# A decoder block's prologue: which engine takes four low parts of the second token block, and where a sum of two weighed conditioning rows stands on GpSimd

## The chip, the cores and the metric

The kernel runs on one core of one Trainium2 chip. A core has TensorE (PE in the profile, its weight loads PEld), VectorE (DVE), ScalarE (ACT), GpSimd (POOL) and SyncE (SP, which here issues the DMA transfers in one queue, in order). The metric is the device time of one execution in microseconds (us), the median of several runs.

## The reference, cut to what matters

```python
mod = jax.nn.silu(c) @ w_cond[l] + b_cond[l]          # c: (1, 1024), w_cond: (1024, 6 * 1024)
shift_m, scale_m, gate_m, shift_f, scale_f, gate_f = [m[:, None, :] for m in jnp.split(mod, 6, axis=-1)]
h = rmsnorm(x, g_mix_pre[l]) * (1.0 + scale_m) + shift_m      # x: (1, 2048, 1024)
proj = h @ w_in[l]                                            # q, k, v: 512 columns each, u: 512
attn = stick_breaking_attention(q, k, v)                      # 8 heads of 64
pool = pooling_mixer(u, w_pool[l], pool_scale[l])             # trailing means over 2, 4, 8, 16 tokens
x = x + gate_m * rmsnorm(concatenate([attn, pool]) @ w_out[l], g_mix_post[l])
h = rmsnorm(x, g_ffn_pre[l]) * (1.0 + scale_f) + shift_f
x = x + gate_f * rmsnorm((silu(h @ w_gate[l]) * (h @ w_up[l])) @ w_down[l], g_ffn_post[l])
```

Everything is float32. The change lies in the first 100 us: in the making of `h` for the second of four blocks of 512 tokens, and in the sums that give the six parts of `mod`.

## The kernel before

**Stages.** A prologue (about 200 us) makes the conditioning parts, turns and modulates the tokens and makes q, k, u and v of the first token blocks; then come the attention with the rest of the projections woven in, the output projection, and the feed-forward part. The order on PE, ACT, DVE and POOL is the order in which the code is written (a manual schedule); SP issues DMAs in order too, each after its own waits, so a DMA that waits holds up those behind it.

**Products in two parts.** A float32 operand x is split into a rounded high part and a low part, x minus the high part. A product takes three passes on PE: high by high, high by low, low by high. `tokens(tb, k)` gives the two parts of token block `tb` for chunk `k`, 128 of the 1024 input columns. For block 1 the parts of chunks 0 to 3 lie in the tile `ht1a` and those of chunks 4 to 7 in `ht1b`.

**Block 1.** `turn1(kc)` has PE turn four 128x128 pieces (L600, tile `x`) and calls `modulate(1, kc, ...)`: ACT writes the high part (L586) and then the unrounded value `h` (L588), and one subtraction makes the low part (L591). Which engine does L591 is the last argument: GpSimd where one is given, else GpSimd for even kc and VectorE for odd. `first_products(n, 1, ...)` multiplies them for the first three chunks of w_in (n = 0, 1, 2: q0, k0, q1): the passes with high parts at L612, those with the low parts at L614. The loop goes over the pairs of chunks (0, 1), (2, 3), (4, 5), (6, 7), and behind each of the first two n it calls `turn1` for a chunk of the next pair, `run_small` (a small task, such as a step of the pooling of `u`) and a step of the conditioning sums.

**Conditioning.** `rest_of_cond` does parts 3, 4, 2 and 5 of `mod`. For each, `cond_sums` loads eight pieces of 128x1024 (`wc`, four buffers, for chunks 0 to 5; two slots of the tile `spare` for chunks 6 and 7), weighs and adds the first six on VectorE (L213 for chunk 0, L215 for the others, into `acc`), and weighs the other two on ACT (L260). GpSimd adds those two into `spare[:, 1]` (L262), 128x1024. `cond_end` runs as a second generator beside the next part's `cond_sums`: it lets two steps pass, adds `spare[:, 1]` into `acc` on VectorE (L271), and goes on to the columns or gate rows.

**Around it on VectorE.** Between the steps stand the first pooling task of `u`: two copies of 16 columns (L376, L377), a sum `us` (L382), and `um` in three instructions (L393, L396, L397). `um` is stored by a DMA from SP (L398, `mtd`); the next load of a `wc` piece is issued behind it in SP's queue.

Of the kernel before, what the change touches and what calls it, by code (L numbers as in the profile page):

```python
# [12 lines left out]
ALU = mybir.AluOpType  # L13
# [7 lines left out]
KC = D // P  # L21
# [22 lines left out]
def block_kernel(ctx, tc, x, c, w_cond, b_cond, g_mix_pre, g_mix_post, w_in, w_pool,  # L44
                 pool_scale, w_out, g_ffn_pre, g_ffn_post, w_gate, w_up, w_down, out):
    nc = tc.nc
# [6 lines left out]
    def raw(ap):  # L53
        return ap.bitcast(F32)
# [151 lines left out]
    def cond_load(part, kc, wc):  # L206
        nc.sync.dma_start(wc, wc_rows[:, kc, part * D:(part + 1) * D])
        return wc

    def cond_step(acc, kc, wc):  # L210

        if kc == 0:
            nc.vector.tensor_scalar_mul(acc, wc, cs[:, 0:1])  # L213
        else:
            nc.vector.scalar_tensor_tensor(acc, wc, cs[:, kc:kc + 1], acc, ALU.mult, ALU.add)  # L215

    def new_wc(name):
        return cond.tile([P, D], F32, tag="wc", bufs=4, name=name)
# [4 lines left out]
    def column_part(acc, part, dst):  # L223
        ps = t_ps(f"cp{part}").rearrange("p (c n) -> p c n", n=64)
        for kc in range(KC):
            nc.tensor.matmul(ps[:, kc], acc[:, kc * P:(kc + 1) * P], ones[:, 0:64],
                             start=True, stop=True)
        nc.vector.tensor_tensor(dst, ps[:, :, 0], colv[:, part * KC:(part + 1) * KC], ALU.add)

    def plus_one_times(dst, g0):  # L230
        nc.vector.scalar_tensor_tensor(dst, dst, 1.0, colv[:, g0:g0 + KC], ALU.add, ALU.mult)

    def gate_part(acc, part, g_post, dst):

        hi, lo = (tokp.tile([P, D], F32R, tag=tag, name=f"gs{part}{tag}") for tag in ("xt", "xs"))
        split(hi, lo, acc)
        g = spare[:, 2 + part // 5]
        nc.sync.dma_start(g, g_post.partition_broadcast(P))
        for _ in range(4):
            yield  # L240
        for half in range(2):
            cols = slice(half * TB, (half + 1) * TB)
            ps = z_ps(f"gp{part}_{half}")
            nc.tensor.matmul(ps, ones_r, hi[:, cols], start=True, stop=False)
            nc.tensor.matmul(ps, ones_r, lo[:, cols], start=False, stop=True)
            nc.vector.tensor_tensor(g[:, cols], g[:, cols], ps, ALU.mult)
        nc.sync.dma_start(dst, g)

    last_sum = {}

    def cond_sums(part, acc):
        if part in (2, 5):
            b = cond.tile([1, D], F32, tag="brow", bufs=1, name=f"br{part}")
            nc.sync.dma_start(b, b_cond[0:1, part * D:(part + 1) * D])
        for n, kc in enumerate((0, 1, 2, 3, 6, 7, 4, 5) if part == 3 else range(KC)):
            wc = cond_load(part, kc, new_wc(f"wc{part}_{kc}") if kc < 6 else spare[:, kc - 6])
            if kc < 6:
                cond_step(acc, kc, wc)
            else:
                nc.scalar.mul(wc, wc, cs[:, kc:kc + 1])  # L260
            if n == KC - 1:
                nc.gpsimd.tensor_tensor(spare[:, 1], spare[:, 1], spare[:, 0], ALU.add)  # L262
                last_sum[part] = spare[:, 1]
            if kc == 0 and part in (2, 5):
                nc.vector.tensor_tensor(acc[0:1, :], acc[0:1, :], b, ALU.add)
            yield

    def cond_end(part, acc):
        yield
        yield  # L270
        nc.vector.tensor_tensor(acc, acc, last_sum.pop(part), ALU.add)  # L271
        for _ in range(1 if part in (2, 5) else 4):
            yield
        if part in (2, 5):
            yield from gate_part(acc, part, *((g_mix_post, gmd) if part == 2 else (g_ffn_post, gfd)))
        else:
            column_part(acc, part, mods["bf" if part == 3 else "af"])
            if part == 4:
                plus_one_times(mods["af"], 56)

    def rest_of_cond():

        end = iter(())
        for part in (3, 4, 2, 5):
            acc = new_acc(part)
            for _ in cond_sums(part, acc):
                next(end, None)
                yield
            for _ in end:
                pass  # L290
            end = cond_end(part, acc)
        for _ in end:
            yield
# [19 lines left out]
    def tokens(tb, k, cols=slice(0, TB)):  # L313
        if tb == 1:
            both = ht[1][k // HK]
            return both[:, 0, k % HK, cols], both[:, 1, k % HK, cols]
        return ht[tb][0][:, k, cols], ht[tb][1][:, k, cols]
# [263 lines left out]
    def modulate(tb, kc, src, low=None):  # L581

        hi, lo = tokens(tb, kc)
        a, b = mods["am"][:, kc:kc + 1], mods["bm"][:, kc:kc + 1]
        h32 = tokp.tile([P, TB], F32, tag="h32", bufs=4, name=f"h{tb}_{kc}")
        nc.scalar.activation(hi, src, AF.Identity, bias=b, scale=a)  # L586
        if tb:
            nc.scalar.activation(h32, src, AF.Identity, bias=b, scale=a)  # L588
        else:
            nc.vector.tensor_scalar(h32, src, a, b, ALU.mult, ALU.add)  # L590
        (low or (nc.gpsimd, nc.vector)[kc % 2]).tensor_tensor(lo, h32, raw(hi), ALU.subtract)  # L591
# [5 lines left out]
    def turn1(kc):  # L597
        pt = t_ps(f"x1_{kc}")
        for j in range(4):
            nc.tensor.transpose(pt[:, j * P:(j + 1) * P], early1[j][:, kc * P:(kc + 1) * P], ident)  # L600
        modulate(1, kc, pt, nc.gpsimd if kc < 3 else None)

    first_ps, lead = {}, []
    first_banks = {(0, 0): mm_only, (3, 0): av_ps, (0, 1): av_ps, (1, 1): mm_only}
# [88 lines left out]
    spare = hc.tile([P, 4, D], F32, tag="hi", name="spare")  # L693
# [9 lines left out]
    first_products(0, 0, 6, 7)  # L703
    first_products(1, 0, 6, 7)
    turn1(0)
    run_small()
    next(rest)
    first_products(2, 0, 6, 7)
    turn1(1)
    run_small()  # L710
    next(rest)
# [5 lines left out]
    for ks in pairs:  # L717
        for n in range(3):
            first_products(n, 1, *ks)
            if n < 2 and ks[0] < 6:  # L720
                turn1(ks[0] + 2 + n)
            run_small()
            if n < 2:
                next(rest)
            if (n, ks[0]) == (0, 6):
                loaded.append(chunk_load(chunks[4], 0))
# [1037 lines left out]
```

## Time and profile before

| what | value |
|---|---|
| median of 3 runs | 2288.1 us (2287.57 to 2288.57) |
| the profiled execution's own time | 2286.46 us, 1.6 us below the median |
| its span in the trace | 2284.5 us, so 2.0 us lie around it |
| mean granted TensorE clock | 0.998 of full speed |
| busy: PE, DVE, ACT, POOL | 2246.8 (98%), 1622.1 (71%), 1164.2 (51%), 1293.0 us (57%) |
| PE busy from 62 to 82 us | 16.48 of 20.00 us |
| PE busy from 82 to 240 us | 157.99 of 158.00 us |

A line of the timeline reads: start in us from the start of the span, duration in us, engine, line of the kernel, operation, output tile <- input tiles, shapes, count, and in brackets the idle time of the engine before it with what ended it. Instructions of one line that follow each other are merged into one row with their count. A line of the list of waits reads: who waited <- for whom, sum in us, times, longest. The chain of work that ended last is a list of start, duration and what was on the chain. Line numbers are those of the kernel before, if not said otherwise; in the kernel after they are smaller by two to four.

### The profile page before, as it was taken

What the parts mean: (1) busy time and instruction counts of PE and PEld (TensorE: products, weight loads), DVE (VectorE), ACT (ScalarE), POOL (GpSimd) and SP (SyncE); (2) the same over time, 40 slices, a digit from 0 to 9 for tenths busy, and PEclk for the clock granted to TensorE, in tenths of its full rate; (3) what the DMA queues carried; (4) which work ended last, traced back from release to release, by engine and by line L of the source; (5) the groups of instructions that cost most, each with busy time, mean ns of one, the idle gap of its engine ahead of it and who ended that gap; (6) DMA issues with size and microseconds to landing.
All of it is one profiled execution on the core that took longest, in us unless ns stands there. A gap on an engine that the chain in (4) does not pass through costs nothing.

```text
span 2284.5 us, 33020 instructions
## 1 busy us (share of the span) xinstructions
PE 2246.8 (98%) x10597; PEld 1842.0 (81%) x10597; DVE 1622.1 (71%) x2243; ACT 1164.2 (51%) x2412; POOL 1293.0 (57%) x1592
## 2 busy tenths in 40 slices
PE   7999999999999999999999999999999999999998
PEld 4788888888888778888888888888888888888886
DVE  7774569999999957666655566787766566655557
ACT  4434569899998855443232323554533323234444
POOL 4342257787778855546777777331576665651004
PEclk9999999999999999999999999999999999999999
DMA  8886764443435536665555555776854333328564
GB/s 313 284 280 204 279 174 117 115 105 105 122 111 158 169 113 220 221 223 171 164 157 161 158 160 185 269 243 206 264 166 131 99 112 96 111 92 301 193 197 143
DMA packets 307081, 405.14 MB, mean 177 GB/s; under 512 B 19222, under 2 KB 179546, under 8 KB 303836
## 3 DMA queue, kind: packets, MB, share of 16 engines
q1 hardware_dynamic: 302444, 400.15, 54.8%
q10 hardware_dynamic: 4464, 2.88, 0.4%
q8 instruction: 83, 1.36, 0.3%
q14 instruction: 90, 0.74, 0.1%
HBM read 274.51 MB, written 128.45 MB: 176 GB/s over the span
## 4 chain that ended last, share of the span: by engine, by line
PE 85%; DVE 9%; DMA 1%; issue 1%; POOL 1%; ACT 1%; SPq 0%; POOLq 0%; DVEq 0%; ACTq 0%
DVE pr L871 5%; PE t_g L68 4%; PE t_u L69 4%; PE t_g L69 4%; PE t_u L68 4%; PE t_g L70 3%; PE t_u L70 3%; PE dn0p L69 3%; PE dn0p L68 3%; PE dn0p L70 3%; PE wt L888 3%; PE dn1p L68 3%; PE dn1p L69 3%; PE dn1p L70 3%; PE b_u L70 3%; PE b_u L69 3%
## 5 line engine op out<-in xcount | busy, mean ns | idle before, releaser
L877 POOL TENSOR_TENSOR w<-sg,pr 128x512 f32<-128x512 f32 (+2 forms) x320 | 307.9, 962 | 38.9 <-DVE pr L871 27.2
L1279 POOL TENSOR_TENSOR s<-s,cu 128x512 f32<-128x512 f32 x88 | 131.4, 1500 | 239.4 <-DVE cu L1278 146.4
L871 DVE TENSOR_TENSOR_SCAN pr<-pr,carry,begin 128x512 f32<-128x512 f32 x192 | 243.6, 1269 | 0.0
L858 ACT ACTIVATE sg<-z 128x512 f32<-128x512 f32 (+2 forms) x320 | 185.0, 578 | 46.8 <-PE z L856 33.2
L59 DVE TENSOR_TENSOR wtl<-wt,wth 128x512 fp32r<-128x512 f32 (+1 forms) x320 | 188.0, 588 | 18.2 <-ACT wth L58 17.9
L58 ACT CAST wth<-wt 128x512 fp32r<-128x512 f32 (+1 forms) x320 | 183.8, 575 | 13.5 <-PE wt L888 13.5
L860 ACT ACTIVATE pr<-z 128x512 f32<-128x512 f32 (+2 forms) x320 | 184.2, 576 | 0.0
L888 PE MATMUL wt<-ident,w 128*128 128x128 f32 x1088 | 174.2, 274 | 4.7 <-POOL pr L868 2.6
L59 DVE TENSOR_TENSOR u_s_l<-u_s,u_s_h 128x512 fp32r<-128x512 f32 x66 | 64.3, 975 | 146.1 <-ACT u_s_h L58 146.1
L888 PEld LDWEIGHTS wt<-ident,w 128*128 128x128 f32 x1088 | 134.7, 140 | 36.8 <-POOL pr L868 3.9
L1269 ACT ACTIVATE s<-s 128x512 f32<-128x512 f32 x88 | 55.7, 633 | 182.2 <-DVE s L1268 182.2
L903 PE MATMUL av<-wth,vt 128*128 128x512 f32 (+1 forms) x320 | 128.9, 403 | 0.8 <-ACT o L908 0.5
L59 DVE TENSOR_TENSOR u_a_l<-u,u_a_h 128x512 fp32r<-128x512 f32 x66 | 73.9, 1121 | 69.3 <-ACT u_a_h L58 69.3
L904 PE MATMUL av<-wtl,vt 128*128 128x512 f32 (+1 forms) x320 | 119.3, 373 | 3.3 <-DVE wtl L59 2.8
L69 PE MATMUL dn0p<-w0p_l,g0p_h 128*128 128x512 f32 x308 | 120.7, 392 | 0.0
L855 PE MATMUL z<-kt,qt 128*128 128x512 f32 (+2 forms) x320 | 118.4, 370 | 2.1 <-ACT pr L860 2.0
L68 PE MATMUL dn0p<-w0p_h,g0p_h 128*128 128x512 f32 x308 | 120.5, 391 | 0.0
L70 PE MATMUL dn0p<-w0p_h,g0p_l 128*128 128x512 f32 x308 | 120.3, 391 | 0.0
L856 PE MATMUL z<-kt,qt 128*128 128x512 f32 (+2 forms) x320 | 117.1, 366 | 0.0
L69 PE MATMUL dn1p<-w1p_l,g1p_h 128*128 128x512 f32 x292 | 114.4, 392 | 0.0
L68 PE MATMUL dn1p<-w1p_h,g1p_h 128*128 128x512 f32 x292 | 114.2, 391 | 0.0
L70 PE MATMUL dn1p<-w1p_h,g1p_l 128*128 128x512 f32 x292 | 114.1, 391 | 0.0
(659 smaller groups left out, 7050.2 us busy)
## 6 DMA issues: line engine op xcount, KB each, us to landing
g<-in_w_gate_dram SPq DMA_DIRECT2D x42, 512.0 KB, 4.7
u<-in_w_up_dram SPq DMA_DIRECT2D x42, 512.0 KB, 5.2
wc<-in_w_cond_dram SPq DMA_DIRECT2D x32, 512.0 KB, 8.1
qt<-qd SPq DMA_DIRECT2D x64, 256.0 KB, 4.0
wd<-in_w_down_dram SPq DMA_DIRECT2D x44, 256.0 KB, 2.9
tdt<-wd SPq DMA_DIRECT2D x44, 256.0 KB, 2.0
w0p<-tdt SPq DMA_DIRECT2D x44, 256.0 KB, 3.5
w1p<-tdt SPq DMA_DIRECT2D x44, 256.0 KB, 2.9
```

Source lines behind the costliest of these rows:

```text
L58: nc.scalar.copy(hi, src)
L59: low.tensor_tensor(lo, src, raw(hi), ALU.subtract)
L68: nc.tensor.matmul(ps, lh, rh, start=first and i == 0, stop=False)
L69: nc.tensor.matmul(ps, lh, rl, start=False, stop=False)
L70: nc.tensor.matmul(ps, ll, rh, start=False, stop=last and i == n - 1)
L858: nc.scalar.activation(sg[:, 0:L], z[:, 0:L], AF.Sigmoid, scale=0.125)
L860: nc.scalar.activation(pr[:, 0:L], z[:, 0:L], AF.Sigmoid, scale=-0.125)
L871: nc.vector.tensor_tensor_scan(pr[:, 0:L][:, ::-1], pr[:, 0:L][:, ::-1], begin[:, TB - L:][:, ::-1], zero if carry is None else carry, ALU ...
L877: nc.gpsimd.tensor_tensor(w[:, 0:L], sg[:, 0:L], pr[:, 1:L + 1], ALU.mult)
L888: nc.tensor.transpose(wt[:, i * P:(i + 1) * P], wss[u][i][:, b * P:(b + 1) * P], ident)
L903: nc.tensor.matmul(av[:, lo0:], vb, wh[:, lo0:], start=first, stop=False)
L1279: nc.gpsimd.tensor_tensor(s, s, u, ALU.mult)
```

## The change

The low part (L591) of every chunk of block 1 but chunk 7 is made by GpSimd: chunks 3 and 5 go over from VectorE. The sum of the two weighed pieces (L262) is no longer written by the last step of `cond_sums` but by the first step of `cond_end`, which runs right behind the first step of the next part.

```diff
@@ -246,8 +246,6 @@
-    last_sum = {}
-
     def cond_sums(part, acc):
...
                 nc.scalar.mul(wc, wc, cs[:, kc:kc + 1])
-            if n == KC - 1:
-                nc.gpsimd.tensor_tensor(spare[:, 1], spare[:, 1], spare[:, 0], ALU.add)
-                last_sum[part] = spare[:, 1]
             if kc == 0 and part in (2, 5):
                 nc.vector.tensor_tensor(acc[0:1, :], acc[0:1, :], b, ALU.add)
             yield
 
     def cond_end(part, acc):
+        nc.gpsimd.tensor_tensor(spare[:, 1], spare[:, 1], spare[:, 0], ALU.add)
         yield
         yield
-        nc.vector.tensor_tensor(acc, acc, last_sum.pop(part), ALU.add)
+        nc.vector.tensor_tensor(acc, acc, spare[:, 1], ALU.add)
...
-        modulate(1, kc, pt, nc.gpsimd if kc < 3 else None)
+        modulate(1, kc, pt, nc.gpsimd if kc != 7 else None)
```

The next two lists are GpSimd's rows from chunk 2 of block 1 on, before and after. `h_2` is the unrounded value of chunk 2 and so on, `spare<-spare` is the sum of the two weighed pieces (of part 3, then of part 4), `wk_0_l` the low part of a weight chunk.

```order
L591 TENSOR_TENSOR ht1a<-h_2_721,ht1a 128x512
L262 TENSOR_TENSOR spare<-spare 128x1024
L591 TENSOR_TENSOR ht1b<-h_4_776,ht1b 128x512
L591 TENSOR_TENSOR ht1b<-h_6_825,ht1b 128x512
L59 TENSOR_TENSOR wk_0_l<-wk_0_32_869,wk_0_h 128x256 x2
L262 TENSOR_TENSOR spare<-spare 128x1024
L59 TENSOR_TENSOR wk_0_l<-wk_0_32_869,wk_0_h 128x256 x2
```

The same place on GpSimd after the change:

```order
L587 TENSOR_TENSOR ht1a<-h_2_721,ht1a 128x512
L587 TENSOR_TENSOR ht1a<-h_3_744,ht1a 128x512
L264 TENSOR_TENSOR spare<-spare 128x1024
L587 TENSOR_TENSOR ht1b<-h_4_776,ht1b 128x512
L587 TENSOR_TENSOR ht1b<-h_5_800,ht1b 128x512
L587 TENSOR_TENSOR ht1b<-h_6_825,ht1b 128x512
L59 TENSOR_TENSOR wk_0_l<-wk_0_32_869,wk_0_h 128x256 x4
L264 TENSOR_TENSOR spare<-spare 128x1024
```

Chunks 3 and 5 came in; part 3's sum now stands behind chunk 3, and part 4's sum behind all four low parts of the weight chunk instead of between them. The sums of parts 2 and 5 keep their places.

VectorE's rows from the last weighed piece of part 3 (`acc_614<-wc_5`) to the third of part 4 (`acc_752<-wc_2`), before:

```order
L215 SCALAR_TENSOR_TENSOR acc_614<-wc_5_729,cs,acc_614 128x1024
L591 TENSOR_TENSOR ht1a<-h_3_745,ht1a 128x512
L376 COPY u_0_705<-halo_230 128x16
L377 COPY halo_230<-u_0_705 128x16
L213 TENSOR_SCALAR acc_752<-wc_0_753,cs 128x1024
L382 TENSOR_TENSOR us_0_1_763<-u_0_705 128x527
L393 SCALAR_TENSOR_TENSOR um_0_780<-us_0_1_763,u_0_705 128x512
L396 TENSOR_TENSOR uf_782<-us_0_1_763,rcnt 128x2
L397 TENSOR_TENSOR um_0_780<-uf_782,u_0_705 128x2
L215 SCALAR_TENSOR_TENSOR acc_752<-wc_1_786,cs,acc_752 128x1024
L591 TENSOR_TENSOR ht1b<-h_5_800,ht1b 128x512
L215 SCALAR_TENSOR_TENSOR acc_752<-wc_2_804,cs,acc_752 128x1024
```

And after:

```order
L215 SCALAR_TENSOR_TENSOR acc_614<-wc_5_729,cs,acc_614 128x1024
L372 COPY u_0_705<-halo_230 128x16
L373 COPY halo_230<-u_0_705 128x16
L213 TENSOR_SCALAR acc_751<-wc_0_752,cs 128x1024
L378 TENSOR_TENSOR us_0_1_763<-u_0_705 128x527
L389 SCALAR_TENSOR_TENSOR um_0_780<-us_0_1_763,u_0_705 128x512
L392 TENSOR_TENSOR uf_782<-us_0_1_763,rcnt 128x2
L393 TENSOR_TENSOR um_0_780<-uf_782,u_0_705 128x2
L215 SCALAR_TENSOR_TENSOR acc_751<-wc_1_786,cs,acc_751 128x1024
L215 SCALAR_TENSOR_TENSOR acc_751<-wc_2_804,cs,acc_751 128x1024
```

The two subtractions are gone and nothing else moved on VectorE: behind these rows stand, as before, the sum into `acc` (L271), the piece `wc_3` of part 4 (L215) and the low part of chunk 7 (L591). PE, ACT and SP have the same rows in the same order.

## The prediction

> **What bounds the kernel now.** First the page's head: PE is busy nearly all the time, so only what makes PE wait counts.
>
> ```profile
> span 2284.5 us, 33020 instructions
> PE 2246.8 (98%) x10597; PEld 1842.0 (81%) x10597; DVE 1622.1 (71%) x2243; ACT 1164.2 (51%) x2412; POOL 1293.0 (57%) x1592
> ```
>
> Then PE's waits up to 240 us, and busy time by stretch (columns: stretch, length, then busy us of PE, PEld, DVE, ACT, POOL, clock, DMA share, GB/s). The change touches the second and third of these waits. After 82 us PE has none for 158 us, so what shifts PE at 82 us shifts all that follows.
>
> ```profile
> PE x_pt L537 <- DVE x_v L119: 5.1, 1, 5.1
> PE first L614 <- DVE ht1a L591: 2.9, 1, 2.9
> PE first L614 <- DVE ht1b L591: 0.6, 2, 0.4
> 62.00:82.00 20.00, 16.48 (x82) 12.62 (x80) 16.21 (x20) 10.67 (x16) 6.95 (x5) 1.00 0.85 295
> 82.00:240.00 158.00, 157.99 (x732) 130.92 (x733) 98.23 (x160) 64.28 (x141) 52.91 (x52) 1.00 0.78 256
> ```
>
> Third, PE's timeline: it waits 2.91 us for chunk 3's low part, 0.40 for chunk 5's, 0.23 for chunk 7's.
>
> ```profile
> 67.48 0.39 PE L614 MATMUL first<-ht1a,wq_h 128*128 128x512 f32 x1
> 70.78 0.50 PE L614 MATMUL first<-ht1a,wq_h 128*128 128x512 f32 x1 [2.91 <-DVE ht1a L591]
> ...
> 76.48 0.50 PE L614 MATMUL first<-ht1b,wq_h 128*128 128x512 f32 x1 [0.40 <-DVE ht1b L591]
> ...
> 81.39 0.39 PE L614 MATMUL first<-ht1b,wq_h 128*128 128x512 f32 x1
> 82.01 0.50 PE L614 MATMUL first<-ht1b,wq_h 128*128 128x512 f32 x1 [0.23 <-DVE ht1b L591]
> ```
>
> Fourth, the chain that ended last, which decides. It does not pass through the 2.91 us wait. It runs from a load of part 4 (issued at 64.64) over VectorE (L213 to L397) to the store of `um`, the load of `wc_3` issued behind that store, its L215 and chunk 7's low part, to PE at 82.01.
>
> ```profile
> 64.64 6.61 DMA wc<-in_w_cond_dram
> 71.28 0.75 DVE acc L213
> ...
> 73.48 1.16 DVE um L397
> 74.66 0.33 SPq L398
> ...
> 75.08 4.25 DMA wc<-in_w_cond_dram
> 79.42 1.37 DVE acc L215
> 81.28 0.69 DVE ht1b L591
> ```
>
> Last, GpSimd and VectorE at that place, and ACT's `h` of chunks 3, 4 and 5.
>
> ```profile
> 66.51 2.37 POOL L262 TENSOR_TENSOR spare<-spare 128x1024 f32<-128x1024 f32 x1
> 73.28 1.33 POOL L591 TENSOR_TENSOR ht1b<-h,ht1b 128x512 fp32r<-128x512 f32 x1 [4.40 <-ACT h L588]
> 78.98 1.29 POOL L591 TENSOR_TENSOR ht1b<-h,ht1b 128x512 fp32r<-128x512 f32 x1 [4.37 <-ACT h L588]
> 68.84 1.28 DVE L215 SCALAR_TENSOR_TENSOR acc<-wc,cs,acc 128x1024 f32<-128x1024 f32 x1 [2.65 <-DMA wc<-in_w_cond_dram]
> 70.04 0.68 DVE L591 TENSOR_TENSOR ht1a<-h,ht1a 128x512 fp32r<-128x512 f32 x1
> 70.91 0.18 DVE L377 COPY halo<-u 128x16 f32<-128x16 f32 x1
> 73.48 1.15 DVE L397 TENSOR_TENSOR um<-uf,u 128x2 f32<-128x2 f32 x1
> 77.55 1.21 DVE L271 TENSOR_TENSOR acc<-acc,spare 128x1024 f32<-128x1024 f32 x1
> 79.42 1.93 DVE L215 SCALAR_TENSOR_TENSOR acc<-wc,cs,acc 128x1024 f32<-128x1024 f32 x1 [0.67 <-DMA wc<-in_w_cond_dram]
> 66.05 0.77 ACT L588 ACTIVATE h<-x,bm,am 128x512 f32<-128x512 f32 x1
> 72.43 0.77 ACT L588 ACTIVATE h<-x,bm,am 128x512 f32<-128x512 f32 x1
> 74.26 0.77 ACT L588 ACTIVATE h<-x,bm,am 128x512 f32<-128x512 f32 x1
> ```
>
> The sum on GpSimd (66.51 to 68.88) fills the time in which VectorE waits for a load until 68.84; there it disturbs nobody.
>
> **The two engines hold each other up.** Rows where they overlap:
>
> ```profile
> 59.15 2.20 DVE L215 SCALAR_TENSOR_TENSOR acc<-wc,cs,acc 128x1024 f32<-128x1024 f32 x1
> 60.63 1.88 POOL L591 TENSOR_TENSOR ht1a<-h,ht1a 128x512 fp32r<-128x512 f32 x1 [0.36 <-ACT h L588]
> 61.87 1.72 DVE L215 SCALAR_TENSOR_TENSOR acc<-wc,cs,acc 128x1024 f32<-128x1024 f32 x1
> 142.10 2.40 POOL L262 TENSOR_TENSOR spare<-spare 128x1024 f32<-128x1024 f32 x1 [1.86 <-ACT spare L260]
> 142.53 2.00 DVE L377 COPY halo<-u 128x16 f32<-128x16 f32 x1 [1.68 <-ACT u L369]
> ```
>
> A copy that takes 0.18 us alone took 2.00 and ended at 144.53, just behind GpSimd's sum (144.50). The L215 of 61.87 ended 1.08 us behind GpSimd's subtraction (62.51); GpSimd's of 60.63 ended 1.16 behind the L215 that ended at 61.35. L397 took 1.15 and ended with chunk 4's subtraction (73.28 + 1.33 = 74.61). So the later one waits for the earlier one's end, then takes 1.08 (L215) or 1.16 (a subtraction), and one that waits goes ahead of the other engine's next. The Trainium skill, SBUF — State Buffer, "Who interferes with whom", says that a VectorE instruction with two SBUF inputs and a GpSimd instruction that reads SBUF block each other for the whole instruction, whichever issues first winning; read strictly, the loser then needs its whole time (1.28, not 1.08), which for the two L215 blocked below would make the forecast some 0.2 us later. The trace has the block and the shorter remainder.
>
> **The change, part by part.**
>
> *Chunk 3 to GpSimd.* Its `h` ends at 66.82, GpSimd is free (66.51), and starts 0.08 later as for chunk 4 (`h` ends 73.20, start 73.28): 66.90, plus 1.3, is 68.21. PE follows 0.06 later, as now (70.72 to 70.78): 68.27 instead of 70.78. Gain at this point 2.51; the wait shrinks to 0.4.
>
> *The sum one place later* starts at 68.17 and ends at 70.54 (2.37). VectorE's L215 of `wc_5`, whose load releases it at 68.84, now meets it and ends at 70.54 + 1.08 = 71.62 instead of 70.12.
>
> *Chunk 4.* PE is 2.51 earlier, so its `h` makes GpSimd ready at 73.28 − 2.51 = 70.77; it waits for that L215, and ends at 71.62 + 1.16 = 72.78. VectorE's first copy of 16 columns waits for that and ends near 72.8.
>
> *Chunk 5 to GpSimd.* Its `h` ends at 75.03 − 2.51 = 72.52, so GpSimd starts at once behind chunk 4 and ends near 74.03. PE reaches this product at 73.57 (76.48 − 0.40 − 2.51) and goes on at 74.09: it is now 2.39 ahead. The second copy, ready at 72.9, waits behind chunk 5 too and ends at 74.06 instead of 71.09.
>
> *The removed subtractions* take 0.68 off VectorE each, the first already in these times, the second between two L215 that have time.
>
> *L213 to L397.* L213 started 0.19 behind the copy because of a load, landed long before now; it starts at 74.0. From its start to L397's start it is 73.48 − 71.28 = 2.20, so L397 starts at 76.2 and ends at 76.37 alone (0.17, as the copies), not 74.63. Chunk 6's subtraction on GpSimd is ready at 78.98 − 2.39 = 76.59, just behind it.
>
> *Store and load.* With L397 1.74 later, the store and `wc_3` go out 1.74 later, at 76.82, and land at 76.82 + 4.25 = 81.07 if the transfer keeps its time. Nothing on SP's queue ahead of them moves. Bounds: at the least the transfer stops mattering and VectorE does: L215 of `wc_1` to 77.6, chunk 6 on GpSimd to 78.73, L215 of `wc_2` to 79.81, L271 to 81.0; so at most 0.1 us is to be won there.
>
> *Chunk 7.* L215 starts 0.09 behind the landing (79.42 against 79.33), at 81.16; without GpSimd beside it it takes 1.28 (now 1.93): 82.44. The subtraction ends 0.60 later (0.68, overlapping 0.08) at 83.04, PE goes on at 83.09 instead of 82.01: **1.1 us later**. PE's 2.39 us of lead end in a wait of 83.09 − (82.01 − 0.23 − 2.39) = 3.7 us.
>
> *Part 4's sum* goes behind two subtractions of a weight chunk, which come earlier by its 2.4 us. VectorE reads it at L271, 12 us later (103.17); PE does not wait there now and will not. I cost it at nothing; what hides it are those 12 us, and if the cover went, its price would be at most its 2.4 us.
>
> Sum: span 2284.5 + 1.1 = 2285.6; own time 2286.46 + 1.1 = 2287.6; against the median, which is 1.6 above the profiled execution, 2288.1 + 1.1 = **2289.2 us**. By the runs shown (2287.57 to 2288.57) the median itself is uncertain by some 0.5. A difference under 0.2% (4.6 us) is about what a measurement of this kernel can tell from no change; all cases below lie within it.
>
> **Rivals.**
>
> *VectorE is not held up, so the kernel is faster.* Were the sum not in its way, L397 would lose the 0.68 of chunk 3 and not be held by chunk 4 (about 1.0): it ends at 73.6, the load lands 1.0 earlier (78.3), L215 ends at 79.6, chunk 7 at 80.25, PE goes on at 80.3: 1.7 us earlier, 2286.4. It turns at 0.66: L215 without GpSimd beside it already wins 0.65, so if L397 ends before 75.3 the kernel is faster. For it speaks that the load of `wc_5` lands only 0.6 us after the sum begins; against it every overlap above.
>
> *The gain of 2.4 stays*, if `wc_3` were not behind the store: 2285.7. The chain shows that it is.
>
> *GpSimd's chunk 6 catches L397*, as chunk 4 does now. It misses it by 0.2 us in my sum; then L397 ends with it at 77.9, and everything is 1.5 us later still: 2290.7.
>
> *PE slows down after the longer wait.* After the first wait of 5.1 us eight turns took 1.97 us, a little later 1.03.
>
> ```profile
> 9.30 1.97 PE L537 MATMUL x_pt<-ident,early_hi 128*128 128x128 f32 x8 [5.07 <-DVE x_v L119]
> 15.72 1.03 PE x_pt L537 x8
> 71.11 0.60 PE L600 MATMUL x<-ident,early_lo 128*128 128x128 f32 x4
> ```
>
> After the wait of 2.91 us four turns took 0.60, so that was too short. Mine is 3.7. If PE then ran at half rate for as long as it had waited, it would lose 1.85: 2291.0. The Trainium skill, TensorE: Matmul & The Clock Gate, Part 1, has the clock halved after an idle window of about 3.4 us that runs freely; an estimate by it is a loss of 1.7 us. The granted clock stands at 1.00 in all these stretches, so the trace shows such a slowing only in the durations.
>
> **How the numbers follow.** Forecast 2289.2: 0.50, its own range 2288.6 to 2289.8. Chunk 6 catches L397, 2290.7: 0.14, since 0.2 us is little. PE slows, 2291.0: 0.07, since the wait is just long enough. VectorE not held, 2286.4: 0.16. Gain kept, 2285.7: 0.08. The rest, 0.05, is what I do not see. From the lowest case to the highest with the median's 0.5 on top at one end and the lowest as it stands: 2285.7 to 2291.2. Over 0.2% either way would need something outside all of these: 0.03 each.
>
> **What the profile of the changed kernel would show.** PE's wait for chunk 3 near 0.4 us and its low product near 68.3; GpSimd's sum from 68.2; the L215 of `wc_5` stretched to some 2.8 us; both copies stretched; L397 ending near 76.4 and the store of `um` behind it; `wc_3` landing near 81; the longest of these PE waits now before chunk 7, near 3.7 us, ended by VectorE. I would be wrong if L215 runs beside the sum in 1.28 us, if L397 ends before 75.3, or if the load, with the queue then fuller or emptier, takes other than 4.25 us.

## The result, and the profile after

| | before | after |
|---|---|---|
| median | 2287.57 us (2285.34 to 2291.54, 17 runs) | 2291.41 us (2288.59 to 2294.24, 17 runs) |
| ratio | | 1.0018, 95% interval 1.0012 to 1.0025 |
| span of the profiled execution | 2284.5 us | 2287.1 us |
| mean granted clock over the runs | 0.9967 (135 runs in all) | 0.9956 (27 runs in all) |

The kernel is slower by 3.8 us between the medians (2.7 to 5.7 by the interval of the ratio). The forecast was 1.1 us more, with a range that ended 3.1 above; the size was missed. The last row counts all runs of these two kernels here, those beside the experiments too. Three runs of the experiments that took about twice the time or more are left out of every number.

From PE's timeline of the kernel after (start, duration, and in brackets the idle time with what ended it). Line numbers are now those of the kernel after; the sum L262 is L264 there, and L213 and L215 keep their numbers.

```profile
67.20 0.39 PE L610 MATMUL first<-ht1a,wq_h 128*128 128x512 f32 x1
67.95 0.51 PE L610 MATMUL first<-ht1a,wq_h 128*128 128x512 f32 x1 [0.36 <-POOL ht1a L587]
...
73.76 0.50 PE L610 MATMUL first<-ht1b,wq_h 128*128 128x512 f32 x1 [0.50 <-POOL ht1b L587]
...
82.50 0.80 PE L610 MATMUL first<-ht1b,wq_h 128*128 128x512 f32 x1 [3.43 <-DVE ht1b L587]
83.09 0.63 PE L608 MATMUL first<-ht1b,wk_h 128*128 128x512 f32 x1
83.52 0.63 PE L608 MATMUL first<-ht1b,wk_l 128*128 128x512 f32 x1
```

The wait of 2.91 us for chunk 3 is now 0.36, and one of 3.43 stands before chunk 7. Behind it the products start 0.59 and 0.43 us apart instead of the 0.34 and 0.23 of before: PE runs at half speed. The first row is the product that stood at 67.48 before, so this execution is 0.28 us early there. Against that, chunk 7 is 0.77 late (82.50 for 82.01).

GpSimd and VectorE at that place:

```profile
66.61 1.28 POOL L587 TENSOR_TENSOR ht1a<-h,ht1a 128x512 fp32r<-128x512 f32 x1 [0.35 <-ACT h L584]
67.85 2.38 POOL L264 TENSOR_TENSOR spare<-spare 128x1024 f32<-128x1024 f32 x1
70.45 3.25 POOL L587 TENSOR_TENSOR ht1b<-h,ht1b 128x512 fp32r<-128x512 f32 x2 [0.22 <-ACT h L584]
76.26 2.09 POOL L587 TENSOR_TENSOR ht1b<-h,ht1b 128x512 fp32r<-128x512 f32 x1 [2.55 <-ACT h L584]
68.33 2.98 DVE L215 SCALAR_TENSOR_TENSOR acc<-wc,cs,acc 128x1024 f32<-128x1024 f32 x1 [2.43 <-DMA wc<-in_w_cond_dram]
71.24 1.26 DVE L372 COPY u<-halo 128x16 f32<-128x16 f32 x1
72.60 1.13 DVE L373 COPY halo<-u 128x16 f32<-128x16 f32 x1
75.84 0.16 DVE L393 TENSOR_TENSOR um<-uf,u 128x2 f32<-128x2 f32 x1
79.36 1.21 DVE L267 TENSOR_TENSOR acc<-acc,spare 128x1024 f32<-128x1024 f32 x1
80.56 1.28 DVE L215 SCALAR_TENSOR_TENSOR acc<-wc,cs,acc 128x1024 f32<-128x1024 f32 x1
81.76 0.68 DVE L587 TENSOR_TENSOR ht1b<-h,ht1b 128x512 fp32r<-128x512 f32 x1
```

L215 takes 2.98 us beside the sum, and both copies are held, as forecast. The L215 of `wc_3` at 80.56 has no bracket: it waits for no load, only for VectorE's own row ahead of it.

The busy time by stretch (columns: stretch, length, then busy us of PE, PEld, DVE, ACT, POOL, clock, DMA share, GB/s) shows the slowing in the granted clock. First the kernel after in its first profile, then the same kernel in a second one:

```profile
82.40:85.80 3.40, 3.30 (x9) 2.63 (x9) 3.09 (x4) 0.59 (x1) 0.00 (x0) 0.50 0.99 318
85.80:89.20 3.40, 3.40 (x25) 3.09 (x24) 0.89 (x3) 1.72 (x3) 0.00 (x0) 1.00 0.99 332
```

```profile
82.40:85.80 3.40, 3.36 (x9) 2.72 (x9) 3.06 (x3) 0.59 (x1) 0.00 (x0) 0.50 1.05 341
85.80:89.20 3.40, 3.40 (x17) 3.40 (x17) 0.75 (x2) 1.65 (x2) 0.00 (x0) 0.50 1.01 321
89.20:92.60 3.40, 3.40 (x11) 2.64 (x11) 0.29 (x2) 0.81 (x3) 0.00 (x0) 0.65 0.29 113
```

PE worked at half speed for 3.4 us in the one and for some 9 in the other. Put beside the kernel before, PE is 0.5 and 0.4 us late at 82 us (by the start of the same instruction), and when the clock is back 2.0 us late in the first, 4.7 in the second. The spans are 2.6 and 5.3 us longer; the last 0.6 us of both arise between 300 and 800 us and are not explained here. The first profile is of one of the shortest executions (2289.36 us, the second shortest of 17); the second (2292.07 us) lies nearer the median.

### The profile page after: what moved, and what is told of

The parts are those of the page before. It is cut to its first block, busy times and chain, and to the rows that moved or that the text cites. A ratio compares the mean times of both kernels' runs of the same rounds, so it can differ in the third digit from the quotient of the medians.

```text
span 2287.1 us, 33019 instructions
## 1 busy us (share of the span) xinstructions
PE 2248.8 (98%) x10597; PEld 1843.1 (81%) x10597; DVE 1619.3 (71%) x2241; ACT 1164.1 (51%) x2412; POOL 1294.7 (57%) x1594
## 4 chain that ended last, share of the span: by engine, by line
PE 81%; DVE 12%; DMA 2%; issue 2%; POOL 2%; ACT 1%; SPq 0%; POOLq 0%; DVEq 0%; ACTq 0%
DVE pr L867 7%; PE t_g L68 4%; PE t_u L69 4%; PE t_g L69 3%; PE t_u L68 3%; PE t_g L70 3%; PE t_u L70 3%; DVE wtl L59 3%; PE dn0p L69 3%; PE dn0p L68 3%; PE dn0p L70 3%; PE dn1p L69 3%; PE dn1p L68 3%; PE dn1p L70 3%; PE b_u L70 3%; PE b_u L69 3%
## 5 line engine op out<-in xcount | busy, mean ns | idle before, releaser
L59 DVE TENSOR_TENSOR wtl<-wt,wth 128x512 fp32r<-128x512 f32 (+1 forms) x320 | 190.7, 596 | 18.7 <-ACT wth L58 18.1
L59 DVE TENSOR_TENSOR u_s_l<-u_s,u_s_h 128x512 fp32r<-128x512 f32 x66 | 65.5, 993 | 144.6 <-ACT u_s_h L58 144.6
L59 DVE TENSOR_TENSOR u_a_l<-u,u_a_h 128x512 fp32r<-128x512 f32 x66 | 73.1, 1109 | 69.7 <-ACT u_a_h L58 69.6
```

The lines of the kernel that those rows point to most:

```text
L59: low.tensor_tensor(lo, src, raw(hi), ALU.subtract)
```

## The experiments

Each was timed in five rounds beside the kernel before; "mean clock" is that of its runs. Line numbers differ by a few between kernels.

**The kernel after once more.**

> The kernel after, once more. Theory (chunk 7's low part about 0.5 to 0.8 us later, and PE at half speed for some 3 us behind the idle wait of 3.4 us, about 1.5 us): 2 to 3 us over the kernel before, ratio near 1.001, PE's wait before chunk 7 again near 3.4 us and the first products behind it again at 0.43 to 0.59 us from start to start instead of 0.23. Rival (the slowing came by chance, and the wait has nothing to do with it): the wait is there again, but the products behind it come every 0.23 us, and the time is about 0.7 us over the kernel before.

Measured: 2291.3 us, ratio 1.0013 (1.0004 to 1.0022). Wait 3.36 us, products behind it 0.59 and 0.43 apart, clock as in the second of the two lists above. The slowing came behind the wait again; the last section shows across all profiles that it belongs to it.

**PE fed in the wait.** Nine products of 128x512 between the low products of chunks 6 and 7.

```diff
+    def feed():
+        idle = t_ps("feed")
+        for _ in range(9):
+            nc.tensor.matmul(idle, loaded[0][1][:, 0, :], tokens(1, 0)[0], start=True, stop=True)
...
+            if (n, ks[0]) == (0, 6):
+                lead.append(feed)
```

> The changed kernel with nine matmuls more (2.0 us of PE work into an unused bank, read by nobody) between the low products of chunk 6 and of chunk 7, so that PE stands idle about 1.4 us there instead of 3.4. Theory (the wait alone makes PE slow afterwards): chunk 7's product starts as late as in the changed kernel (0.5 to 0.8 us later than before), but the matmuls behind it keep their 0.39 us and the span comes out about 1.6 us below the changed kernel's, 0.8 above before's. Rival (PE's slow stretch behind 82 us is not due to the wait): the matmuls behind chunk 7 still take 0.8 us, the span is that of the changed kernel (+2.6) or longer.

Measured: 2289.88 us, ratio 1.0010 (1.0001 to 1.0019), mean clock 0.9966, as the kernel before. The wait left is 1.64 us, and the products behind it come every 0.23 us: no slowing. Yet the time is 2.65 us over the kernel before. In the profile PE is 0.7 us late at 82 us and 1.8 from 134 us on. Three rows show where the second part arises, one on ACT and two of PE's list of waits (from 60 to 240 us):

```profile
90.68 0.59 ACT L58 CAST q<-first 128x512 fp32r<-128x512 f32 x1 [3.21 <-DMA qd<-q]
```

```profile
PE first L610 <- DVE ht1b L587: 1.6, 1, 1.6
PE u L68 <- DVE q L59: 0.7, 1, 0.7
```

SP's order is not written by hand, and with the extra products it came out otherwise: the store of q behind a load of a weight chunk (issued at 80.93). That store, issued at 84.57, landed 6.0 us later; in the kernel before such stores took 3.1 to 3.6. So q is late (90.68; 87.10 in the kernel before), and at 134 us PE waits for VectorE's low part of a later q. The kernel before has no such wait, but not by much:

```profile
129.78 1.23 DVE L59 TENSOR_TENSOR gs2xs<-acc,gs2xt 128x1024 fp32r<-128x1024 f32 x1
130.93 0.68 DVE L59 TENSOR_TENSOR q<-q,q 128x512 fp32r<-128x512 f32 x1
```

```profile
132.28 0.39 PE L68 MATMUL u<-ht1a,wu_h 128*128 128x512 f32 x1
```

VectorE is done at 131.61, 0.67 us ahead of PE. I had missed this second place.

**Without part 3's sum** (part 3 then lacks two of its eight pieces):

```diff
     def cond_end(part, acc):
-        nc.gpsimd.tensor_tensor(spare[:, 1], spare[:, 1], spare[:, 0], ALU.add)
+        if part != 3:
+            nc.gpsimd.tensor_tensor(spare[:, 1], spare[:, 1], spare[:, 0], ALU.add)
```

> The changed kernel without the sum of the two weighed pieces of part 3 on GpSimd (this part of the computation is left out). Theory (the sum holds up VectorE, and VectorE's own work then makes chunk 7's low part late): L215 of wc_5 takes 1.28 us instead of 2.98, L393 ends about 1.1 us earlier, chunk 7's product starts near 81.4 instead of 82.50, PE waits 2 us for it and keeps its speed; span about 2.7 us below the changed kernel's, within 0.5 of before's. Rival (the two copies held by chunks 4 and 5 are enough): chunk 7 as late as in the changed kernel, span +2.6 over before.

Measured: 2288.38 us, ratio 1.0008 (0.9999 to 1.0017). Chunk 7 at 82.39 us: hardly earlier. VectorE's rows:

```profile
73.17 1.77 DVE L379 TENSOR_TENSOR us<-u 128x527 f32<-128x527 f32 x1
75.86 3.52 DVE L215 SCALAR_TENSOR_TENSOR acc<-wc,cs,acc 128x1024 f32<-128x1024 f32 x2
80.44 1.28 DVE L215 SCALAR_TENSOR_TENSOR acc<-wc,cs,acc 128x1024 f32<-128x1024 f32 x1
```

With the sum gone, chunk 5's subtraction meets `us` (1.77 us instead of 0.70), chunk 6's again the second of the two L215, and VectorE reaches `wc_3` at 80.44 instead of 80.56. But the load of `wc_5` also landed 1.5 us later in this profile than in that of the kernel after (69.85 for 68.33), so that L215, now 1.28 us long, ended at 71.13 and not much before the 71.31 of the kernel after. What the sum costs by itself is therefore not shown; that another collision came up where one was taken away is. PE's wait of 2.65 us was followed by half speed, too.

**The parts of the change alone**, and chunk 7 added (each line as it is with the edit):

```diff
# sum at its old place, chunks 3 and 5 to GpSimd; and the change with chunk 7 as well
+        modulate(1, kc, pt, nc.gpsimd if kc != 7 else None)
+        modulate(1, kc, pt, nc.gpsimd)
# the sum one step later, chunks 3 and 5 on VectorE
+        modulate(1, kc, pt, nc.gpsimd if kc < 3 else None)
```

> Chunks 3 and 5 to GpSimd, the sum at its old place ahead of chunk 3. Theory: the sum runs while VectorE waits for its load, as before, so L215 of wc_5 is not held, but chunk 3's low part comes only behind the sum and that L215: PE goes on between 70.2 and 71.4 instead of 70.8; L393 ends earlier than before (about 73.8), chunk 7 no longer waits long; PE is 0 to 1 us behind before at 85 us; if the wait for chunk 3 grows to 3.5 us, PE may slow there too (1.6 us more). Rival (GpSimd's subtraction is slower, that alone is the loss): the same loss as in the changed kernel, +2.6, with the wait in front of chunk 7.

Measured: 2288.46 us, ratio 1.0007 (0.9998 to 1.0015). Chunk 3 waits behind the sum (3.26 us, slowed behind it), chunk 5 1.4, none for chunk 7, 0.6 at 134 us.

> Only the sum's move, chunks 3 and 5 left on VectorE; on GpSimd only part 4's sum then moves, behind the four low parts of the weight chunk. Theory (part 4's sum costs nothing): within 0.3 us of the kernel before, PE's waits of 2.9 and 0.4 us for chunks 3 and 5 as before, chunk 7 at 82.0 us, no slowing. Rival (part 4's sum, later, holds VectorE or the conditioning part behind it): a new wait of PE between 84 and 135 us, and 1 to 2.4 us over the kernel before.

Measured: 2287.8 us, ratio 0.9999 (0.9990 to 1.0008): part 4's sum costs nothing that can be seen. Its wait of 2.75 us for chunk 3 was followed by half speed; that of 2.91 in the kernel before was not.

> The changed kernel with chunk 7 on GpSimd as well, so that it no longer stands behind VectorE's L215 of wc_3. Theory: GpSimd makes it between two L215, by about 80.6; PE goes on near 80.7 instead of 82.5, with a wait of 1.6 us and no slowing; span 3.4 us below the changed kernel's, about 1 below before's. Rival (GpSimd has too much now): chunk 7's low part after 82, span at or over the changed kernel's.

Measured: 2288.24 us, ratio 1.0004 (0.9995 to 1.0013), mean clock 0.9977. Chunk 7 at 80.84 us behind 1.54 us, no slowing: PE is 1.2 us ahead of the kernel before. It does not stay ahead (waits after 84 us):

```profile
PE u L68 <- DVE k L59: 2.0, 2, 1.1
PE u L68 <- DVE q L59: 1.0, 1, 1.0
```

By the last of these, at 134.85 us, PE is 2.6 us behind.

**The store of `um` from ACT's queue.**

```diff
-            nc.sync.dma_start(mtd[tb][4 + g], m)
+            (nc.scalar if tb == g == 0 else nc.sync).dma_start(mtd[tb][4 + g], m)
```

> The kernel after, with the store of the first um issued from ScalarE's queue, so that the load of wc_3 isn't behind it. Theory (in the kernel after VectorE's own row of instructions, wc_1, wc_2 and the sum into acc, ends at 80.58 us, with the load 0.1 us ahead of that): wc_3 lands some us earlier, yet its weighing still starts near 80.5, chunk 7's low product within 0.2 us of 82.5 behind a wait near 3.4 us, and the time is that of the kernel after. Rival (the store and the load behind it set the time, as the chain of the kernel before has it): the weighing of wc_3 starts 1 us earlier or more, chunk 7 at 81.5 us, a wait near 2.4 us, 1 us or more less than the kernel after.

Measured: 2291.81 us, ratio 1.0020 (1.0011 to 1.0029). It tells little: ACT waited 5.12 us at the store, chunk 5's high part behind it came late, and PE waited 3.75 us for that instead, and slowed. The weighing of `wc_3` started at 79.73 us, 0.8 earlier, because chunk 5 no longer met the second copy. That the load doesn't set chunk 7 rests on the row at 80.56 above.

**High products first** in the kernel before: all three products with high parts of a pair ahead of those with low parts.

```diff
+            first_products(n, 1, *ks, low=False)     # then turn1, run_small, next(rest) as before
+        for n in range(3):
+            first_products(n, 1, *ks, high=False)
```

> The kernel before, where PE does the products with high parts of all three chunks of w_in for a pair ahead of those with low parts, so that it has work while a low part is missing. Theory (VectorE's chain is right behind PE at 87, 111 and 134 us, with about 0.6 us of slack at 134): the waits of 2.9, 0.4 and 0.2 us between 62 and 82 us shrink by 1.5 us or more together, PE is 1 to 2 us ahead at 84 us, waits for the low parts of q and k at 87 to 135 us, and 0 to 0.6 us remain, 2286.6 to 2287.3 us if the kernel before is at 2287.2. Rival (what shifts PE at 82 us shifts all that follows, as I predicted): the lead stays, 1 to 2 us faster than before.

Measured: 2290.12 us, ratio 1.0010 (1.0001 to 1.0019). The wait for chunk 3 fell to 1.5 us, but q's store went out late here too (SP's order changed), and PE waited 3.15 us for a low part of k at 87 us and slowed behind it. Neither answer was settled, as the store order had changed as well.

**One small product in the middle of the wait.** SP's order stays. In the kernel after it reads the sum into `acc` of part 3, in the kernel before GpSimd's sum:

```diff
+    def feed():
+        idle = t_ps("feed")
+        nc.tensor.matmul(idle[:, 0:64], part_acc[3][:, 0:P], ones[:, 0:64], start=True, stop=True)
```

> The kernel after, with one extra product of 128x64 on PE between the low products of chunks 6 and 7, which reads VectorE's sum into acc and so runs near 80.6 us: it cuts PE's wait of 3.4 us in two of about 1.6 and 1.9 us, and adds 0.1 us of work. Theory (PE slows only behind one unbroken wait of more than some 2.5 us): the products behind chunk 7 come every 0.23 us again, the mean granted clock over the runs is that of the kernel before, 0.9967, or above, and the time lies 0.5 to 1.2 us over the kernel before (chunk 7 is still 0.5 to 0.8 us late). Rival (it is the idle time in all, however it is cut): the slowing stays, mean clock near 0.9955, 3 us or more over the kernel before.

Measured: 2290.58 us, ratio 1.0014 (1.0005 to 1.0023), mean clock 0.9963. In the profile the wait is cut and the clock stays at 1.00, but PE, 0.5 us late at 82, is 1.7 late at 134:

```profile
80.75 0.41 PE L717 MATMUL feed<-ones,acc 128*128 128x64 f32 x2 [1.67 <-DVE acc L267]
82.50 0.50 PE L613 MATMUL first<-ht1b,wq_h 128*128 128x512 f32 x1 [1.35 <-DVE ht1b L590]
...
133.99 0.50 PE L68 MATMUL u<-ht1a,wu_h 128*128 128x512 f32 x1 [1.05 <-DVE q L59]
```

So in this execution taking the slowing away uncovers VectorE's lateness. It is the second shortest of the 11 (2287.77 us); the median is 2.5 us over that of the kernel before beside it, and the mean clock is below 0.9967, so others of the runs did slow.

> The kernel before, with one extra product of 128x64 on PE between the low products of chunks 2 and 3, which reads GpSimd's sum of part 3 and so runs near 69 us: it cuts PE's wait of 2.9 us in two of about 1.1 and 1.8 us. Theory (the kernel before also slows behind its 2.9 us in many of its runs, though not in the one whose profile I had): chunk 3 still at 70.8 us, mean clock 0.9975 or more where the kernel before has 0.9967, and 1 to 2 us faster than it. Rival (2.9 us is too short to slow PE, and the runs of the kernel before lose their clock elsewhere): mean clock 0.9967, time within 0.4 us of the kernel before.

Measured: 2285.97 us, ratio 0.9996 (0.9987 to 1.0005), mean clock 0.9971. Between the two theories: the median is 2.1 us under that of the kernel before beside it, while the ratio gives only 0.9.

**VectorE relieved ahead of 134 us**: the low part of part 2's gate sum (L59, `gs2xs`) on GpSimd. By the same line that of part 5 goes over as well.

```diff
-        split(hi, lo, acc)
+        split(hi, lo, acc, nc.gpsimd)
```

> The kernel after with the extra product that cuts PE's wait before chunk 7, and with the low part of part 2's gate sum (128x1024, 1.23 us on VectorE, straight ahead of the low part of q for which PE waits 1.05 us at 134 us) on GpSimd. Theory (what the slowing left over is VectorE's chain, which is late at 134 us because q's store, and the loads behind it, went out late at 84 to 92 us): the wait at 134 us falls under 0.2 us, PE stays 0.5 to 0.8 us behind the kernel before from 82 to 240 us instead of 1.7, and the time is about 1 us under that of the kernel with the extra product alone. Rival (something else holds PE at 134 us, or GpSimd now does): a wait of 0.5 us or more remains between 130 and 145 us, and the time is that of the kernel with the extra product alone, 2 us or more over the kernel before.

> The kernel after with the extra product and the gate sum's low part on GpSimd, once more. Theory: where the clock holds, PE is 0.5 to 0.8 us behind the kernel before from 82 to 240 us, with no wait over 0.2 us at 134 us; mean clock near 0.9967; 0.3 to 1.5 us over the kernel before. Rival (the first result was luck): 2 to 3 us over, as with the extra product alone, and a wait of 0.5 us or more at 134 us.

Measured: ratios 1.0002 (0.9993 to 1.0011) and 1.0008 (0.9999 to 1.0017), medians 2287.87 and 2290.13 us, mean clocks 0.9967 and 0.9956. No wait at 134 us in either profile. But PE slowed in both, although its wait was cut into 1.66 and 1.46 us in the first, 1.65 and 1.56 in the second. The first of them:

```profile
78.90:82.40 3.50, 0.92 (x5) 0.39 (x3) 3.43 (x4) 0.00 (x0) 0.00 (x0) 0.94 1.00 380
82.40:85.80 3.40, 2.86 (x7) 2.30 (x8) 3.09 (x4) 0.59 (x1) 0.00 (x0) 0.50 1.02 327
85.80:89.20 3.40, 3.40 (x18) 3.31 (x16) 1.17 (x2) 1.63 (x2) 0.00 (x0) 0.50 0.96 313
```

A theory of mine falls here: an unbroken wait isn't needed. Two waits of 3.1 us in all, with one small product between them, do it too.

> The kernel after with the low part of part 2's gate sum on GpSimd, and nothing else: the wait of 3.4 us before chunk 7 and the slowing behind it stay, VectorE's chain at 134 us is relieved. Theory (the slowing hides VectorE's lateness, so that either alone leaves most of the loss): mean clock near 0.9955 as in the kernel after, 2 to 4 us over the kernel before, against 0.9 with the extra product as well; PE 2 us or more behind the kernel before from 90 us on, no wait at 134 us. Rival (VectorE's chain was the whole loss): within 1 us of the kernel before, whatever the clock.

Measured: ratio 1.0009 (1.0000 to 1.0018), median 2290.3 us, mean clock 0.9957. In the profile the wait of 3.5 us and a slowing of 3.4 us are there, PE is 2.35 us behind from 84 us on, and no wait follows. The runs fall apart: five with a clock of 0.996 and above at 2286.6 to 2289.3 us, five below at 2291.3 to 2292.5.

> The kernel before with the extra product that cuts PE's wait of 2.9 us, and with the low part of part 2's gate sum on GpSimd. Theory: PE's wait of 0.8 us at 132.7 us goes, PE is 0.4 to 0.8 us ahead of the kernel with the extra product alone from there on, mean clock 0.997 or above, and the time is 1 to 2 us under the kernel before: the fastest of all versions. Rival (the wait is given back further on, or GpSimd's longer subtraction delays the weight chunk behind it): no more than 0.3 us from the kernel with the extra product alone.

> The kernel before with the extra product and the gate sum's low part on GpSimd, once more. Theory: no wait at 132 us, mean clock 0.997 or above, and 1 to 2 us under the kernel before, the interval now clear of it. Rival: within 0.5 us of the kernel before.

Measured: ratios 0.9991 (0.9982 to 1.0000) and 0.9991 (0.9983 to 1.0000), 2285.93 and 2285.71 us: 1.7 and 1.9 us under the kernel before, the fastest version here, with intervals that end at 1.

**What the change costs at the same clock.** The runs of a kernel, sorted by their granted clock (median us, number of runs; the few at 0.999 and those at 0.994 are left out):

| granted clock | before | after | after, gate sum on GpSimd | before, extra product and gate sum |
|---|---|---|---|---|
| 0.998 | 2286.6 (27) | none | 2287.0 (9) | 2285.6 (9) |
| 0.997 | 2287.2 (28) | 2289.5 (7) | 2287.8 (6) | 2285.8 (3) |
| 0.996 | 2287.9 (70) | 2290.7 (5) | 2289.3 (3) | 2286.9 (7) |
| 0.995 | 2289.3 (6) | 2292.1 (11) | 2290.6 (5) | 2287.6 (1) |

The fourth column is the two kernels after with the gate sum on GpSimd, with and without the extra product. At the same clock the change costs 2.3 to 2.8 us. That a clock of the same mean costs more here fits the place of the slowing. Besides 82 us, the profiles have slowings at 26, 44 and 795 us, the kernel before too at 795. In the execution of the fed kernel PE was slowed at 26 us, too: it was 0.65 us late at 29.5 us, and level with the kernel before at 32.1, since it waits there anyway. The slowing at 82 us meets no wait that would take it up: 0.77 for chunk 7 and 1.5 for 3.4 us at half speed are 2.3 us. Of the 3.6 us between the means of all runs (2287.7 and 2291.25) some 2.6 come at an equal clock, and some 1.0 from the lower clock, which fits executions in which the slowing lasts longer; that is argued, since only two executions have a profile.

With VectorE relieved the kernels after lie 0.4 to 1.4 us over the kernel before as it was, but 1.4 to 3.0 over the one with the same edit and the extra product. So the gate sum is not what sets the kernels apart. In the kernel after it is worth about 1.5 us at the same clock, though no profile of that kernel has a wait at 134 us. In its first profile PE goes from 2.0 us behind the kernel before at 240 us to 2.6 at the end; with the gate sum on GpSimd it goes from 2.35 to 1.9 (both executions at a clock of 0.997). So at least part of this gain lies behind 240 us, and its cause stays open.

## Why the prediction was wrong

Its sum held nearly row by row (the forecast times less 0.28 us are to be compared):

| step | forecast | after |
|---|---|---|
| PE goes on at chunk 3 | 68.27, wait 0.4 | 67.95, wait 0.36 |
| the sum on GpSimd | 68.17 to 70.54 | 67.85 to 70.23 |
| L215 of `wc_5` ends | 71.62 | 71.31 |
| chunk 5 ends, second copy ends | 74.03, 74.06 | 73.70, 73.73 |
| store of `um` ready (L397, now L393) | 76.37 | 76.00 |
| `wc_3` weighed from | 81.16 | 80.56 |
| PE goes on at chunk 7 | 83.09, 1.1 late, wait 3.7 | 82.50, 0.77 late, wait 3.43 |

- *Chunk 7.* The load of `wc_3` was issued 1.74 us later than before by the forecast; SP issued it at 76.46 (forecast 76.82). It landed in time, so VectorE's own row set the start, the bound that the prediction gave with "at most 0.1 us to be won".
- *The failed step: the weight of a rival.* "PE slows down after the longer wait" had 0.07 and came true, in every profile in which the wait before chunk 7 was 2.65 us or more and unbroken. In the sum of the forecast the slowing stands at nothing. Its price in the rival was 1.85 by the rule "half rate for as long as it had waited"; it was 1.5 (3.4 us at half speed) in one execution and 4.2 (some 9 us) in another, more than the 0.77 of the chunk itself. The prediction took 2.91 us without a slowing, seen once, as a limit. The kernel with only the sum moved slowed behind 2.75, and the last section shows why the 2.91 passed. The prediction also held that the trace shows a slowing only in the durations; the stretches above show it in the granted clock.
- *The range.* It was to reach from the lowest case to the highest with 0.5 on top, but its end, 2291.2, is the 2290.7 of chunk 6 with 0.5; the highest case, 2291.0, would have given 2291.5.
- *A second step, false but hidden: "What shifts PE at 82 us shifts all that follows."* It was argued from PE's list of waits, which has none for 158 us. But VectorE's low part of q is only 0.67 us ahead of PE at 132 us: the kernel with the wait cut went from 0.5 to 1.7 us late there, and the lead of 1.2 us at 81, with chunk 7 on GpSimd, was 2.6 us of lag at 135. For the change itself this step cost nothing, and that is luck: a PE slowed by 1.5 us arrives late enough, and in the profile after VectorE is done there at 133.42, 0.9 us ahead of PE. Without the slowing the forecast would have missed a wait of 1.05 us there, as the kernel with the wait cut shows. How VectorE becomes late I read from SP's order (q's store, behind it `b_cond` and the next part's loads); that was not tested by itself.
- *Part 4's sum at nothing*: right (0.9999). *Chunk 6 catches L397*: it started 0.26 us behind it; forecast 0.2, rightly not the main case. *VectorE not held*, *the gain of 2.4 stays*: didn't happen. *Faster, same, slower*: the change is 0.18% slower, within the bound of 0.2%.

What stays open is what puts VectorE at 134 us later in one kernel than in another, and what the gate sum gains behind 240 us. An interval here reaches some 2 us either way, so the ratios 1.0018, 1.0013 (the kernel after, twice) and 1.0014 (with the extra product) can't be told apart.

## What to carry to other kernels

When waits of PE are moved about, price not their sum but the longest one and what lies close around it: waits of 2.9, 0.4 and 0.2 us cost nothing beside themselves in the profile before, while 0.4, 0.5 and 3.4 us brought 1.5 to 4.2 us of slower products with them. One profile without a slowing is no proof that a wait is short enough: it may be the lucky execution. A list of waits without an entry doesn't say that nothing is close: read for each engine by how much it is ahead of PE at the next places where PE depends on it, before a gain or a loss is carried to the end. And with two engines that hold each other up, taking one collision away can bring up another, as it did here in the run without part 3's sum.

## What the runs showed of the hardware

Whether PE slows behind a wait differs between executions and isn't set by the wait's length alone. Between 62 and 90 us half speed followed behind single waits of 2.65, 2.75, 3.15, 3.26, 3.36, 3.43, 3.5 and 3.75 us, but not behind 2.91, nor behind any up to 1.64. Of waits cut in two, 1.66 with 1.46 and 1.65 with 1.56 slowed PE and 1.67 with 1.35 did not; 1.07 with 1.25 did in one profile of three.

The traces show what decides. In each profile the granted clock changes only at the ends of intervals of 3.413 us that follow each other without a gap (in the profile after at 82.39, 85.80, 795.78 and 799.19 us), and each execution has them at another place in the kernel's work. From 62 to 92 us, in all 17 profiles, half speed began behind every interval in which PE stood idle for 2.08 us or more (11 profiles), and behind none with 1.72 or less. In the kernel before the wait of 2.91 us fell on two intervals, with 1.19 and 1.72 us idle. In the kernel after PE was idle for 3.32 us of the interval up to 82.39 in the first profile, and for 2.29 of the one up to 81.37 in the second. By these two bounds an estimate is that a single wait of 2.91 us slows PE in 63 to 84% of the executions and one of 3.43 us in 79 to 100%, if the intervals can lie anywhere; by it the profile before was of the rarer, lucky kind.

The same intervals tell how long a slowing lasts. Full speed came back behind a slow interval with at most 0.56 us idle, and not behind one with 0.60 or more, with one kind of exception. In the second profile after, the interval from 81.37 still held 1.07 us of the wait. The next one, mostly taken by the 16 small products of L226, did not bring full speed back either, though PE was never idle in it; the third did, at 91.61. So idle time is not the whole measure: at 26.76 us of the same profile half speed began behind an interval with 0.32 us idle, which held small products of 128x64 and 1x64.

The Trainium skill, TensorE: Matmul & The Clock Gate, Part 1, has a window of 3413 ns that runs freely, and half speed after an idle one. The trace agrees with the length and with the free running; that 2.08 us of idle time in an interval can be enough, and that a slowing can last 10.2 us (81.37 to 91.61), the runs add.

The mean clock of a kernel's runs counts slow intervals wherever they lie: 0.9977 with chunk 7 on GpSimd too, 0.9967 before, 0.9956 after. It doesn't tell their place: the fed kernel has 0.9966, though no wait above 1.64 us was left between 62 and 84 us in its profile.
